# ConvFFN: tiles 2 to 20 of each half issued in a written-out order, with products summed in PSUM

## The chip, the cores and the metric

The kernel runs on one core of one Trainium2 chip. The metric is device time: microseconds from the first to the last instruction of one execution, as the median of several runs. A second number appears throughout, the span of one execution that the hardware profiler recorded.

## What is computed

The reference is a two-layer backbone over 1024 latent tokens of width 1024 and, in layer 0, 256 context tokens. Layer 0 mixes by Fourier transforms and a gated MLP, layer 1 by neighbourhood attention; both then run the same ConvFFN, which is where the change lies:

```python
def conv_ffn(h, w_up, conv_w, conv_b, w_down):
    L = h.shape[1]
    a = h @ w_up
    gate, val = a[..., :D_FF], a[..., D_FF:]
    gp = jnp.pad(gate, ((0, 0), (CONV_W // 2, CONV_W // 2), (0, 0)))
    g = gp[:, 0:L] * conv_w[0] + gp[:, 1:1 + L] * conv_w[1] + gp[:, 2:2 + L] * conv_w[2] + conv_b
    return (jax.nn.silu(g) * val) @ w_down
```

`D_FF` is 2816, the convolution is three wide, and layer 0 applies the ConvFFN to latent and context tokens, layer 1 to latent tokens alone. Everything is float32.

## The kernel before

**Precision.** Every float32 matrix is split into a high part (a copy rounded to the matmul's type, made on ScalarE, L447) and a low part (the difference, L448, on VectorE or, where the caller asks, on GpSimd). A product of two matrices is then three matmuls: high by high, high by low, low by high (`PASSES`).

**Halves and tiles.** The tokens of a layer are worked in two halves: in layer 0 two times 320 and two times 324 columns, in layer 1 two times 256 and two times 258. So there are four halves in the program, called the first to the fourth here. For each half the 22 tiles of 128 channels of `D_FF` follow each other (f = 0 to 21). The two-column-block product `h @ w_up` is done by a scheme with seven products P1 to P7 in place of eight. Each is 12 matmuls (four depths, three passes) with weight combinations called A00, A01, A11, S1 to S4 and operand combinations that were made before the half begins. After the products, their sums give four blocks: C0 = (c00, c01), the gate, and C1 = (c10, c11), the value.

**One tile.** `up` issues, for tile f: the seven products (L306), each into a PSUM bank of its own from a pool of eight named `pq`; a copy of P1 to SBUF on ScalarE (L323); seven additions on VectorE that take a product out of PSUM (L311); then `gate` (L315 on ScalarE, the outer taps of the convolution L317 and L319 on VectorE, silu L321 on ScalarE); the multiplication by the value (L361, VectorE); and the split of the result `act` (L447 and L448). Between the products stand four calls of `down` (L376), the second matrix multiplication for the pair of tiles before, with its accumulation into the residual stream (L382, VectorE). In a half of 256 columns a `down` is six matmuls 512 wide, in the others twelve.

**Weights.** The weights of tile f+1 are prepared while tile f runs. Two 512 KB loads (L236, queue of SyncE) bring A00 and A01 in one buffer, A10 and A11 in the other; these `wr` buffers are two in all, so that the loads for tile f+2 wait until all that is left in them of tile f+1 has been read. GpSimd forms the combinations in place: L241 (S1 = A10 + A11, needs both halves of the second load), L247 (S3 = A00 - A10), L248 (S2 = S1 - A00, overwrites A00) and L251 (S4 = A01 - S2). Each of the seven then gets its high part on ScalarE and its low part on VectorE, except A00, A01 and A11, whose low parts GpSimd makes too (`POOL`). Each weight has one slot in SBUF, which comes free when its product of tile f is done: A00 and S2 share the tile `wh` of one number, S1 and S4 that of another; A01, S3 and A11 are `wq`. `prep` does the same for the weights of `down` (`wd`).

**What sets the order.** The program is written in one order and put into another by a planner that simulates the engines and issues by priority. The sums, the gate and the split of `act` run at high priority. The planner's order is then fixed for each engine: each engine works through its own list, and waits where an operand is not there. During tiles 1 to 3 of a half further work lies between the products (`BESIDE`): in the first half of each layer the normalization of the second half's columns, one step being a VectorE instruction (L152), a ScalarE one (L153) and a store to DRAM (L176, `nd`) from one shared buffer; in layer 0's second half sums of squares.

## Time and profile before

| what | value |
|---|---|
| median of three runs | 2914.65 us (2911.54 to 2923.23) |
| the profiled execution's own time | 2920.99 us |
| its span | 2919.1 us |
| granted TensorE clock, mean | 0.974 |
| busy share: PE, PEld, DVE, ACT, POOL | 95%, 86%, 76%, 45%, 43% |
| gate (L315) of tile 2 in the four halves | 552.6, 1003.0, 2171.4, 2557.0 us |
| gate of tile 20 in the four halves | 911.3, 1363.4, 2479.2, 2877.7 us |

PE is TensorE's matmuls, PEld its weight loads, DVE VectorE, ACT ScalarE, POOL GpSimd, SP SyncE. Busy times of PE are modelled at their ends, so a PE that is always busy need not be at its peak. A row of the timeline gives start, duration, engine, line, output and inputs; a bracket gives the idle time before it and what ended it. A tile's period is the distance between two executions of L315, of which each tile has one: 88 in all.

### The profile page before, as it was taken

What the parts mean: (1) busy time and instruction counts of PE and PEld (TensorE: products, weight loads), DVE (VectorE), ACT (ScalarE), POOL (GpSimd) and SP (SyncE); (2) the same over time, 40 slices, a digit from 0 to 9 for tenths busy, and PEclk for the clock granted to TensorE, in tenths of its full rate; (3) what the DMA queues carried; (4) which work ended last, traced back from release to release, by engine and by line L of the source; (5) the groups of instructions that cost most, each with busy time, mean ns of one, the idle gap of its engine ahead of it and who ended that gap; (6) DMA issues with size and microseconds to landing.
All of it is one profiled execution on the core that took longest, in us unless ns stands there. A gap on an engine that the chain in (4) does not pass through costs nothing.

```text
span 2919.1 us, 47590 instructions
## 1 busy us (share of the span) xinstructions
...
## 2 busy tenths in 40 slices
...
GB/s 303 215 189 118 98 217 72 112 74 86 80 87 101 75 80 87 73 81 87 24 169 101 137 109 183 180 179 80 37 109 101 95 87 98 105 89 93 94 88 95
DMA packets 335886, 327.67 MB, mean 112 GB/s; under 512 B 16217, under 2 KB 264617, under 8 KB 335657
## 3 DMA queue, kind: packets, MB, share of 16 engines
...
## 4 chain that ended last, share of the span: by engine, by line
PE 61%; DVE 14%; DMA 7%; POOL 7%; issue 5%; ACT 5%; SPq 0%; POOLq 0%; DVEq 0%; ACTq 0%
PE pq L306 18%; PE pq L478 15%; PE pq L376 11%; PE ps L478 6%; DMA wr<-in_ffn_w_up_dram 4%; POOL ws L241 2%; DVE xl L382 2%; DVE wh L448 2%; PE pq L566 2%; POOL wh L448 2%; DVE hx L311 2%; PE ps L487 2%; ACT t L1227 1%; POOL wr L248 1%; DMA wd<-in_ada_w_dram 1%
## 5 line engine op out<-in xcount | busy, mean ns | idle before, releaser
L376 PE MATMUL pq<-act,wd 128*128 128x320 f32 (+3 forms) x3696 | 639.8, 322 | 59.3 <-DVE xl L382 24.5
L376 PEld LDWEIGHTS pq<-act,wd 128*128 128x128 f32 x3696 | 557.1, 193 | 92.0 <-DVE xl L382 28.7
L306 PE MATMUL pq<-hs,wh 128*128 128x320 f32 (+3 forms) x4128 | 607.5, 299 | 16.3 <-DVE xl L382 7.8
L306 PEld LDWEIGHTS pq<-hs,wh 128*128 128x128 f32 x4128 | 576.9, 191 | 26.4 <-DVE xl L382 11.2
L306 PE MATMUL pq<-hs,wq 128*128 128x320 f32 (+3 forms) x3144 | 469.8, 299 | 8.4 <-DVE wq L448 4.9
L478 PE MATMUL pq<-hs,wh 128*128 128x512 f32 (+3 forms) x2100 | 469.0, 358 | 3.6 <-DVE hs L724 1.9
L306 PEld LDWEIGHTS pq<-hs,wq 128*128 128x128 f32 x3144 | 442.5, 191 | 14.1 <-DVE wq L448 5.7
L478 PEld LDWEIGHTS pq<-hs,wh 128*128 128x128 f32 x2100 | 365.8, 193 | 78.0 <-issue 6.2
L241 POOL TENSOR_TENSOR ws<-wr 128x512 f32<-128x512 f32 x88 | 153.6, 1745 | 397.3 <-DMA wr<-in_ffn_w_up_dram 333.0
L447 ACT ACTIVATE wh<-wr 128x512 fp32r<-128x512 f32 (+1 forms) x223 | 161.8, 726 | 354.0 <-POOL wr L248 201.5
L382 DVE SCALAR_TENSOR_TENSOR xl<-pq,mod,xl 128x320 f32<-128x320 f32 (+5 forms) x616 | 304.1, 514 | 11.7 <-PE pq L376 11.6
L448 DVE TENSOR_TENSOR wh<-wr,wh 128x512 fp32r<-128x512 f32 (+1 forms) x147 | 166.9, 1135 | 184.8 <-ACT wh L447 184.5
L448 POOL TENSOR_TENSOR wq<-wr,wq 128x512 fp32r<-128x512 f32 x152 | 235.7, 1550 | 32.9 <-ACT wq L447 32.9
L478 PE MATMUL ps<-hs,wh 128*128 128x512 f32 x840 | 240.0, 405 | 3.6 <-ACT hs L721 1.8
L311 DVE TENSOR_TENSOR hx<-hx,pq 128x320 f32<-128x320 f32 (+3 forms) x440 | 196.1, 448 | 29.1 <-PE pq L306 21.6
L447 ACT ACTIVATE wq<-wr 128x512 fp32r<-128x512 f32 x262 | 160.0, 623 | 101.3 <-PE pq L306 73.2
L447 ACT ACTIVATE wh<-ws 128x512 fp32r<-128x512 f32 x172 | 107.5, 625 | 169.8 <-PE pq L306 115.4
L478 PEld LDWEIGHTS ps<-hs,wh 128*128 128x128 f32 x840 | 141.9, 191 | 41.6 <-issue 14.4
L251 POOL TENSOR_TENSOR ws<-wr 128x512 f32<-128x512 f32 x88 | 120.2, 1366 | 123.3 <-DVE wh L448 112.3
L999 POOL TENSOR_TENSOR hsp<-hsq,hsp 128x512 fp32r<-128x512 f32 (+1 forms) x40 | 47.1, 1185 | 265.5 <-ACT hsq L998 265.5
L1006 DVE RECIPROCAL hsq<-hsq 128x512 f32<-128x512 f32 (+1 forms) x40 | 121.1, 3030 | 52.9 <-ACT hsq L1005 52.1
L448 DVE TENSOR_TENSOR wd<-wrd,wd 128x512 fp32r<-128x512 f32 x176 | 155.5, 912 | 0.2 <-ACT wd L447 0.2
...
## 6 DMA issues: line engine op xcount, KB each, us to landing
wr<-in_ffn_w_up_dram SPq DMA_DIRECT2D x176, 512.0 KB, 4.4
...
adaw<-in_ada_w_dram SPq DMA_DIRECT2D x128, 256.0 KB, 3.6
...
```

The costliest lines, as they stand in the source:

```text
L241: op(raw["S1"], raw["A10"], raw["A11"], ALU.add)
L251: op(x, raw["A01"], raw["S2"], ALU.subtract)
L306: nc.tensor.matmul(o, w[wn][:, wp, k], self.part(s, bn, k, sp), start=(k == 0 and i == 0), stop=(k == 3 and i == 2))
L311: nc.vector.tensor_tensor(o, x, y, ALU.add)
L376: nc.tensor.matmul(pd, self.wds[j][i][:, wp, d % 4], self.acts[f][:, sp, lo:lo + m], start=(i == 0 and pi == 0), stop=(i == len(fs) - 1 an ...
L382: nc.vector.scalar_tensor_tensor(x, pd[:, a - lo:b - lo], net.mod[:, self.layer, st, 5, d:d + 1], x, ALU.mult, ALU.add)
L447: self.nc.scalar.activation(h, src, AF.Copy)
L448: return (e or self.nc.vector).tensor_tensor(l, src, f32(h), ALU.subtract)
L478: nc.tensor.matmul(o, w(wp, k), s(k, sp), start=(ki == 0 and pi == 0), stop=(ki == len(order) - 1 and pi == 2))
L487: nc.tensor.matmul(out, l[a], r[b], start=(first and i == 0), stop=(last and i == 2))
L566: nc.tensor.matmul(acc[32 * q:32 * q + 32, 0:256], self.sT[:, k, :], w[q // 2][:, 256 * (q % 2):256 * (q % 2) + 256], start=(k == 0), stop ...
L1006: nc.vector.reciprocal(r, r)
```

## The change

Tiles 2 to 20 of each half are taken out of the planner's hands for four engines (PE, DVE, ACT, POOL): inside the region each engine's list is the order in which the code issues, and that is read off a tuple of names, `STEADY` (or `STEADY2` for tile 2). The DMA queue of SyncE is not in the region. Inside it:

- P6 accumulates into P1's bank, P7 and (from tile 3) P4 go on in that bank, and P3 goes on in P5's. The running sums are copied out by ScalarE where they are wanted (`U`, `V`, `c10`), and three VectorE additions (`c00+`, `c11+`, `c01+`) are left of seven; tile 2 has four.
- The end of a tile (silu, multiplication, split of `act`) moves into the next tile, as do the last two accumulations of `down` (`X2`, `X3`): a name with a minus is work of the tile before.
- `D0` to `D3` are the matmuls of `down`, `X0` to `X3` their accumulations; `wA00` and so on are the steps of the weights. S1's parts are made before S2's, and the two loads stand behind S3's and A11's.
- A00's low part moves from GpSimd to VectorE.
- Tiles 0, 1 and 21 stay with the planner; the work beside tiles 2 and 3 is issued at its place between the products.

```diff
-    POOL = ("A00", "A01", "A11")
+    POOL = ("A01", "A11")
+    STEADY = ("P1", "silu-", "X2-", "X3-", "P2", "c00", "mul-", "wA00", "P6", "acth-", "c00+", "actl-", "wA01", "P5",
+              "U", "P7", "prep", "D0", "V", "wS1", "c11+", "P4", "wS2", "X0", "D1", "c10", "wS3", "wload0", "P3", "wA11",
+              "wload1", "X1", "D2", "c01+", "gate", "wS4", "taps", "D3", "ws")
+    STEADY2 = ("P1", "silu-", "P2", "c00", "mul-", "wA00", "P6", "acth-", "c00+", "actl-", "wA01", "P5",
+               "U", "P7", "prep", "V", "wS1", "c11+", "P4", "wS2", "c10+", "D0", "wS3", "wload0", "P3", "X0", "wA11",
+               "wload1", "D1", "c01+", "gate", "wS4", "X1", "D2", "taps", "D3", "ws")
...
+        def product(p, onto=None):
             wn, bn = self.PROD[p]
-            o = net.t(net.ps, [P, 512], "pq" if p in ("P2", "P5") else "pq")[:, :n]
+            o = net.t(net.ps, [P, 512], "pq")[:, :n] if onto is None else onto
             for k in range(4):
                 for i, (wp, sp) in enumerate(PASSES):
-                    nc.tensor.matmul(o, w[wn][:, wp, k], self.part(s, bn, k, sp), start=(k == 0 and i == 0),
-                                     stop=(k == 3 and i == 2))
+                    nc.tensor.matmul(o, w[wn][:, wp, k], self.part(s, bn, k, sp),
+                                     start=(onto is None and k == 0 and i == 0), stop=(k == 3 and i == 2),
+                                     skip_group_check=onto is not None)
...
+        if steady:
+            onto = dict(P6="P1", P7="P6", P3="P5")
+            if f > 2:
+                onto["P4"] = "P7"
+            ops = {"c00": lambda: copy(c00, x["P1"]), "c00+": lambda: add(c00, c00, x["P2"]),
+                   "U": lambda: copy(c01, x["P6"]), "V": lambda: copy(c10, x["P7"]),
+                   "c11+": lambda: add(c11, c10, x["P5"]), "c10": lambda: copy(c10, x["P4"]),
+                   "c10+": lambda: add(c10, c10, x["P4"]), "c01+": lambda: add(c01, c01, x["P3"]),
+                   "gate": gate, "taps": taps, "prep": prep}
+            i = 0
+            for tok in self.STEADY if f > 2 else self.STEADY2:
+                if tok in self.PROD:
+                    x[tok] = product(tok, x[onto[tok]] if tok in onto else None)
+                    if i in beside:
+                        beside[i]()
+                    i += 1
+                elif tok[0] == "D":
+                    adds["X" + tok[1]] = downs[int(tok[1])]()
+                elif tok[-1] == "-":
+                    if tok[:-1] in before:
+                        before[tok[:-1]]()
+                elif tok[0] == "X":
+                    adds.pop(tok)()
...
+            self.before = dict(after, **adds)
+            return
...
             for f in range(NF):
-                ups.append(self.up(s, f, hooks, [lambda d=d, j=f - 2: self.down(s, j, j % 2 * 4 + d) for d in range(4)]
+                if f == 2:
+                    region = self.net.tc.manual_schedule(engines={engines.PE, engines.DVE, engines.Activation, engines.Pool})
+                    region.__enter__()
+                if f == NF - 1:
+                    region.__exit__(None, None, None)
```

In the changed kernel the lines are: products L317, copies L326, additions L323, gate L329, taps L335 and L337, split of `act` L342 and L346, silu L347, multiplication L348, matmuls of `down` L437, accumulations L447, high and low parts of weights L523 and L524, GpSimd's sums L248, L254, L255 and L258.

**GpSimd, tile 14 of the fourth half.** Here stand the weights for the next tile; `ws` is S1 and then S4, `wr` the two raw buffers. Before:

```order
L241 TENSOR_TENSOR ws_27610<-wr_27556 128x512
L247 TENSOR_TENSOR wr_27556<-wr_27520,wr_27556 128x512
L448 TENSOR_TENSOR wh_20746<-wr_27520,wh_20746 128x512
L448 TENSOR_TENSOR wq_20648<-wr_27520,wq_20648 128x512
L248 TENSOR_TENSOR wr_27520<-ws_27610,wr_27520 128x512
L251 TENSOR_TENSOR ws_27610<-wr_27520 128x512
L448 TENSOR_TENSOR wq_20973<-wr_27556,wq_20973 128x512
```

After:

```order
L248 TENSOR_TENSOR ws_27275<-wr_27237 128x512
L254 TENSOR_TENSOR wr_27237<-wr_27221,wr_27237 128x512
L255 TENSOR_TENSOR wr_27221<-ws_27275,wr_27221 128x512
L524 TENSOR_TENSOR wq_20466<-wr_27221,wq_20466 128x512
L258 TENSOR_TENSOR ws_27275<-wr_27221 128x512
L524 TENSOR_TENSOR wq_20791<-wr_27237,wq_20791 128x512
```

Between the sum that gives S3 (L247, now L254) and the one that gives S2 (L248, now L255) stood two low parts, A00's (`wh`) and A01's (`wq`); now none stands there.

**VectorE, the end of tile 14 of the fourth half and the start of tile 15.** `hx` holds C0 and C1, `g` the gate, `xl` the residual stream. Before:

```order
L311 TENSOR_TENSOR hx_27616<-hx_27616,pq_27762 128x258
L448 TENSOR_TENSOR wh_20747<-ws_27610,wh_20747 128x512
L382 SCALAR_TENSOR_TENSOR xl_3274<-pq_27780,mod_127,xl_3274 128x256
L382 SCALAR_TENSOR_TENSOR xl_3274<-pq_27788,mod_127,xl_3274 128x258
L317 SCALAR_TENSOR_TENSOR g_27617<-hx_27616,cols_175_786,g_27617 128x515
L382 SCALAR_TENSOR_TENSOR xl_3409<-pq_27796,mod_127,xl_3409 128x256
L382 SCALAR_TENSOR_TENSOR xl_3409<-pq_27804,mod_127,xl_3409 128x258
L319 SCALAR_TENSOR_TENSOR g_27617<-hx_27616,cols_175_786,g_27617 128x515
L448 TENSOR_TENSOR wd_27866<-wrd_27668,wd_27866 128x512
L448 TENSOR_TENSOR wd_27869<-wrd_27668,wd_27869 128x512
L361 TENSOR_TENSOR g_27617<-g_27617,hx_27616 128x516
```

After:

```order
L323 TENSOR_TENSOR hx_27277<-hx_27277,pq_27334 128x258
L524 TENSOR_TENSOR wh_20565<-ws_27275,wh_20565 128x512
L335 SCALAR_TENSOR_TENSOR g_27278<-hx_27277,cols_175_786,g_27278 128x515
L337 SCALAR_TENSOR_TENSOR g_27278<-hx_27277,cols_175_786,g_27278 128x515
L447 SCALAR_TENSOR_TENSOR xl_3274<-pq_27440,mod_127,xl_3274 128x256
L447 SCALAR_TENSOR_TENSOR xl_3274<-pq_27447,mod_127,xl_3274 128x258
L447 SCALAR_TENSOR_TENSOR xl_3409<-pq_27460,mod_127,xl_3409 128x256
L447 SCALAR_TENSOR_TENSOR xl_3409<-pq_27467,mod_127,xl_3409 128x258
L348 TENSOR_TENSOR g_27278<-g_27278,hx_27277 128x516
L524 TENSOR_TENSOR wh_20564<-wr_27420,wh_20564 128x512
L323 TENSOR_TENSOR hx_27476<-hx_27476,pq_27496 128x258
L346 TENSOR_TENSOR act_27527<-g_27278,act_27527 128x516
```

The accumulations of the last two `down`s have moved behind both taps, the low parts of `wd` away from this place, and A00's low part (`wh_20564`) in behind the multiplication.

**ScalarE, the start of tile 15 of the fourth half, after the change.**

```order
L347 ACTIVATE g_27278<-g_27278 128x516
L326 ACTIVATE hx_27476<-pq_27478 128x258
L523 ACTIVATE wh_20564<-wr_27420 128x512
L342 ACTIVATE act_27527<-g_27278 128x516
L523 ACTIVATE wq_20466<-wr_27420 128x512
L326 ACTIVATE hx_27476<-pq_27478 128x258
```

The copy of P1 (first L326) stands behind silu of tile 14, and the copy of P1 + P6 (second L326) behind A00's high part, the high part of `act` and A01's high part. The matmuls of P6 write the bank that the first reads, those of P7 the bank that the second reads.

71 lines of the change are left out of this document (49 added, 22 removed).

## The prediction

> **What bounds the kernel now.** I first read the table of busy times by stretch. The stretches run from gate to gate: tile 2 of the first half, then tiles 4 to 19 of the first half and 3 to 19 of the others.
>
> ```profile
> core 0: us, PE busy (x) PEld busy (x) DVE busy (x) ACT busy (x) POOL busy (x), PEclk, DMA share, GB/s
> 552.60:579.50 26.90, 21.90 (x141) 20.85 (x140) 26.90 (x48) 12.44 (x24) 11.49 (x9) 0.98 0.36 104
> 599.80:911.30 311.50, 309.96 (x2109) 309.52 (x2108) 285.38 (x497) 128.18 (x208) 173.59 (x112) 1.00 0.27 82
> 1029.10:1363.40 334.30, 333.92 (x2237) 331.39 (x2237) 304.45 (x528) 137.99 (x223) 183.10 (x119) 1.00 0.27 81
> 2190.40:2479.20 288.80, 272.99 (x1848) 251.11 (x1847) 225.14 (x360) 123.94 (x221) 175.88 (x119) 0.98 0.32 94
> 2576.60:2877.70 301.10, 277.94 (x2233) 274.91 (x2232) 231.40 (x427) 125.84 (x223) 195.51 (x121) 0.98 0.30 90
> ```
>
> In layer 0 (second and third row) PE hardly has a gap: 309.96 of 311.50 us and 333.92 of 334.30. A tile takes 311.50 / 16 = 19.47 and 334.30 / 17 = 19.66 us there, and nothing that spares other engines can shorten it. In layer 1 a tile takes 288.80 / 17 = 16.99 and 301.10 / 17 = 17.71 us, and PE has gaps. Its floor there comes from stretches of the chain of waits in which PE alone runs, first the third half, then the fourth:
>
> ```profile
> 2303.33 2.79 PE pq L376 x12
> 2306.13 5.69 PE pq L306 x48
> ```
>
> ```profile
> 2752.82 5.79 PE pq L306 x48
> ```
>
> Third half: 84 x 5.69 / 48 + 24 x 2.79 / 12 = 9.96 + 5.58 = 15.54 us. Fourth: (84 + 48) x 5.79 / 48 = 15.92 us. The gap to the present periods, 1.45 and 1.79 us, times 17 tiles each, is 24.7 + 30.4 = 55 us: about all that the change can win in its long run of tiles.
>
> What holds layer 1 up is seen in the chain of waits of the fourth half, one lap of it:
>
> ```profile
> 2769.24 4.80 DMA wr<-in_ffn_w_up_dram
> ...
> 2774.17 3.44 POOL ws L241
> ...
> 2779.29 1.74 POOL wh L448
> 2781.03 0.06 POOL wq L448
> 2781.08 1.16 issue
> 2782.24 1.30 POOL wr L248
> ...
> 2787.30 4.94 DMA wr<-in_ffn_w_up_dram
> ```
>
> It is the weights' loop: load, GpSimd's sums, high part, low part, and the next load waits for the buffer. A lap is 2787.30 - 2769.24 = 18.06 us, the period of a tile. PE waits at its end for VectorE, which waits in its list for S2's high part.
>
> A second limit is less visible. GpSimd and VectorE shut each other out:
>
> ```profile
> 2765.63 1.27 POOL L251 TENSOR_TENSOR ws<-wr 128x512 f32<-128x512 f32 x1
> 2766.25 1.20 DVE L448 TENSOR_TENSOR wh<-wr,wh 128x512 fp32r<-128x512 f32 x1 [4.34 <-ACT wh L447]
> 2767.34 1.28 POOL L448 TENSOR_TENSOR wq<-wr,wq 128x512 fp32r<-128x512 f32 x1 [0.43 <-ACT wq L447]
> 2768.49 0.68 DVE L448 TENSOR_TENSOR wq<-wr,wq 128x512 fp32r<-128x512 f32 x1
> ```
>
> GpSimd's sum ends at 2766.90 and the low part that had begun at 2766.25 ends 0.55 us later; GpSimd's next ends at 2768.62, the other low part again 0.55 us later. So a low part needs 0.55 us with GpSimd kept out, and is held until GpSimd's running instruction (some 1.15 of its 1.28 us) is over. VectorE's additions out of PSUM show nothing of this (row of L311 below).
>
> The Trainium skill has the rule ("SBUF — State Buffer", Who interferes with whom): a VectorE instruction with two SBUF inputs contends with a GpSimd instruction that reads SBUF, by an exclusive lock. It speaks against this change, which takes off VectorE four additions that never collide and puts on one low part that does; the rows above agree, and what it would cost here is worked out, from rows, in the second and third rival.
>
> **The change, part by part.** TensorE's work is unchanged: as many matmuls, in fewer banks.
>
> *The loop.* Between S3's and S2's sums on GpSimd stood A00's and A01's low parts: 1.74 + 0.06 + 1.16 = 2.96 us of the lap. Both are gone from there, so the lap falls to 18.06 - 2.96 = 15.10 us, under the floor of 15.92. GpSimd's list loses 1.74 us of 195.51 / 17 = 11.5.
>
> *VectorE in layer 1.*
>
> ```profile
> L311 DVE TENSOR_TENSOR hx<-hx,pq 128x258 f32<-128x258 f32 x85 | 35.2, 414 | 1.2
> L448 DVE TENSOR_TENSOR wh<-ws,wh 128x512 fp32r<-128x512 f32 x35 | 30.7, 876 | 0.3 <-ACT wh L447 0.2
> L448 DVE TENSOR_TENSOR wh<-wr,wh 128x512 fp32r<-128x512 f32 x18 | 21.5, 1194 | 62.0 <-ACT wh L447 62.0
> L448 DVE TENSOR_TENSOR act<-g,act 128x516 fp32r<-128x516 f32 x17 | 16.8, 987 | 5.1 <-ACT act L447 5.1
> ```
>
> ```profile
> L315 ACT ACTIVATE g<-hx,cols,cols 128x516 f32<-128x516 f32 x17 | 13.9, 820 | 50.6 <-DVE hx L311 50.6
> L447 ACT ACTIVATE wh<-ws 128x512 fp32r<-128x512 f32 x35 | 21.9, 625 | 13.3 <-PE pq L306 6.5 <-POOL ws L241 6.2 <-POOL ws L251 0.6
> ```
>
> Busy now 231.40 / 17 = 13.61 us a tile in the fourth half. Four additions go (4 x 0.414 = 1.66), a low part comes (0.68): 12.63. New is a hole: between `c01+` and S4's low part nothing stands in VectorE's list, and it waits there for gate and S4's high part, 0.82 + 0.625 = 1.44 us: 14.07 with the collisions of today. Of those today's busy time holds about 2 x 0.20 + 0.51 + 0.31 = 1.2 us (the three means above less 0.68). Six GpSimd instructions remain; if none shut VectorE out it needs 12.9 us, if each did for its whole 1.15 us, 14.07 + 6.9 - 1.2 = 19.8. With half of that it needs 16.3, and in the third half (13.24 busy now) 16.0. Both lie just over PE's floor. I take the middle between floor and present period, 16.27 and 16.82 us, since two lists that are both nearly full also wait for each other: a gain of 0.72 and 0.89 us, times 17: **12.3 + 15.2 = 27.5 us**. The ends are 55 (floor) and nothing or a loss (rivals).
>
> ScalarE gets three copies more, 0.42 us each at most, on 125.84 / 17 = 7.4 us of a tile: covered in sum, but two of them are now waited for by PE. Before, a product went into a bank of its own; now P6 must wait until P1 is copied, P7 until P1 + P6 is.
>
> *Layer 0.* The price of that wait is a chain from the end of P3 to the start of P6 in the next tile: `c01+`, gate, S4's high and low part, four taps, silu, copy. Its rows, second half:
>
> ```profile
> L311 DVE TENSOR_TENSOR hx<-hx,pq 128x324 f32<-128x324 f32 x85 | 41.5, 488 | 10.1 <-PE pq L306 7.4
> L361 DVE TENSOR_TENSOR g<-g,hx 128x648 f32<-128x648 f32 x17 | 31.5, 1854 | 0.0
> L319 DVE SCALAR_TENSOR_TENSOR g<-hx,cols,g 128x131 f32<-128x131 f32 x17 | 15.5, 912 | 0.0
> L319 DVE SCALAR_TENSOR_TENSOR g<-hx,cols,g 128x515 f32<-128x515 f32 x17 | 14.8, 868 | 0.0
> L317 DVE SCALAR_TENSOR_TENSOR g<-hx,cols,g 128x515 f32<-128x515 f32 x17 | 12.7, 747 | 0.0
> L317 DVE SCALAR_TENSOR_TENSOR g<-hx,cols,g 128x131 f32<-128x131 f32 x17 | 6.0, 350 | 0.0
> ```
>
> ```profile
> 1003.05 0.93 ACT L315 ACTIVATE g<-hx,cols,cols 128x648 f32<-128x648 f32 x1 [0.71 <-DVE hx L311]
> 1009.92 0.75 ACT L321 ACTIVATE g<-g 128x648 f32<-128x648 f32 x1 [2.57 <-DVE g L319]
> 1013.69 0.42 ACT L323 ACTIVATE hx<-pq 128x324 f32<-128x324 f32 x1
> ```
>
> 0.49 + 0.93 + 0.63 + 0.68 + (0.75 + 0.87 + 0.35 + 0.91) + 0.75 + 0.42 = 6.78 us, and some 0.3 for seven handovers. What PE does meanwhile are D2, D3, P1 and P2, 48 x 333.92 / 2237 = 7.17 us. So the copy arrives as PE wants it, with nothing to spare. VectorE's sum there, 304.45 / 17 = 17.91 - 4 x 0.488 + 0.68 + 1.55 = 18.2 us, stays under 19.66; the slow row of L361 (1854 ns for 648 columns, where 512 of a low part take 680) shows that collisions of today, one of 1.0 us at least, are in it. I put 0.1 us a tile for chance meetings, 33 tiles: **+3 us**, from below zero by a few us (PE has no gap to give) up to the rival.
>
> *Tile 2 of the first and third half.* The normalization's steps stand fixed between the products and share one buffer, so each waits for the store of the one before:
>
> ```profile
> 555.17 0.72 ACT L153 ACTIVATE act<-act,mod 128x512 f32<-128x512 f32 x1 [1.08 <-DVE act L152]
> DMA to landing us min/median/max: 1.5/2.1/3.8
> ```
>
> After a step VectorE may do the next only 0.72 + 0.3 (issue) + 2.1 = 3.1 us later. Written between them are 1.2 us (`c00+`, `act`'s low part), 2.5 (two of `wd`, S1, `c11+`) and 1.9 (S2, `c10+`, S3): (3.1 - 1.2) + (3.1 - 2.5) + (3.1 - 1.9) = 3.7 us of waiting. VectorE is busy throughout that tile now (26.90 of 26.90), so it comes in full. Twice, and rounded up: **+8 us**; ends: nothing, if the planner's own order lost as much, and 5 x 3.1 in each, 31.
>
> **Sum.** -27.5 + 3 + 8 = -16.5 us. The profiled execution took 2920.99 us, 6.3 over the median of the runs; less 16.5 it would be 2904.5, and on the median's scale 2914.65 - 16.5 = **2898 us**.
>
> **Rivals.** *The tiles reach PE's floor*: GpSimd's instructions fall into VectorE's holes (the hole after `c01+` is one that fits), and nothing waits. For it: the lap of 15.1 is under the floor. Against it: VectorE's 14 to 16 us of 15.9. Time: 2914.65 - 55 + 8 = 2868.
>
> *A new wait of the same length*: in layer 1 VectorE, shut out, is late with `c01+`, silu comes late, PE stands before P6, P7 or D3 (whose bank waits for `c01+`) as long as it stood before `down`. For it: S1's and S2's low parts follow GpSimd's sums closely, as the row of 1194 ns shows for today. Time: 2914.65 + 8 + 3 = 2926, within 0.5% of before. Whether it or the forecast comes true hangs on the phases of the two lists, which no row shows.
>
> *Slower: layer 0's chain runs over.* The chain to P6 has nothing to spare, and `c01+` stands in the list behind S3's low part and `X1`. If GpSimd meets one more instruction of the chain than today's rows hold, by half its length, 0.58 us, every one of 33 tiles loses that: 19 us, with nothing won in layer 1 and 8 us in the tiles 2: 2914.65 + 27 = 2942. It decides once the chain takes longer than 7.2 us. For it: L361's 1854 ns, which shows GpSimd there; against it: GpSimd has one instruction less, and the multiplication is no part of this chain.
>
> **How the numbers follow.** Forecast (half of layer 1's gap) 0.33, floor reached 0.19, new wait of the same length 0.22, layer 0 longer 0.26. About 0.5% of this kernel, 15 us, is what a measurement tells from no change. Faster by more: the floor and most of the forecast (0.28), 0.47. Within: the rest of the forecast and the same-length wait, 0.05 + 0.20 = 0.25. Slower: 0.28. The forecast's own range is 2880 to 2915; with floor and longer chain it is 2852 to 2943.
>
> **What would show it.** Right: periods of L329 of 16.0 to 16.6 us in the third half and 16.4 to 17.2 in the fourth; GpSimd's wait for the load before the first sum still there, the wait of ScalarE for S2's sum gone; gaps of PE before L317 ended by the copies L326. Layer 0's tiles at 19.4 to 19.8. L159 waiting for stores `nd` in tile 2 of the first and third half. Wrong: layer 0 at 20 us or more (the chain), or layer 1 at 17 or more (the same wait under another name), or a period at 15.6 and 15.9 (floor).

## The result: 72 us slower, and the profile after

The changed kernel takes 2987.42 us (median of 4 runs, 2981.65 to 2989.14) against 2914.9 us before (4 runs beside it, 2911.54 to 2923.23): a ratio of 1.0241, with a 95% interval of 1.0215 to 1.0267. The forecast was 2898, its widest range 2852 to 2943. The profiled execution took 2989.14 us, span 2987.2 us, 68.1 more than before.

Where they came from is read from the gates of the profiled executions, four entries (gate of tile 0 to gate of tile 4) and four steady runs of 16 tiles (gate of tile 4 to gate of tile 20):

| stretch | before | after | difference |
|---|---|---|---|
| entries of the four halves, us | 80.6, 73.2, 65.1, 61.7 | 87.2, 86.2, 75.2, 66.6 | +34.6 |
| steady tile, layer 0, first and second half, us | 19.47, 19.73 | 20.66, 20.80 | +36.2 |
| steady tile, layer 1, third and fourth half, us | 17.13, 17.74 | 17.22, 17.36 | -4.6 |
| all else | | | +1.9 |

So three things want explaining: layer 0 lost a microsecond a tile, layer 1 won nothing, and each entry lost 5 to 13 us. First the busy times by stretch (columns as in the prediction), gate to gate in the long runs of the four halves, of the changed kernel:

```profile
611.10:941.70 330.60, 314.21 (x2114) 309.95 (x2113) 293.30 (x448) 137.66 (x256) 139.77 (x96) 1.00 0.26 77
1066.70:1423.10 356.40, 338.65 (x2246) 333.99 (x2245) 313.30 (x476) 148.24 (x274) 148.50 (x102) 1.00 0.25 76
2253.70:2546.70 293.00, 268.79 (x1837) 246.76 (x1836) 268.52 (x308) 137.37 (x273) 145.07 (x102) 1.00 0.31 92
2651.80:2946.50 294.70, 277.12 (x2252) 271.82 (x2251) 269.68 (x375) 137.56 (x273) 150.73 (x102) 1.00 0.30 90
```

In layer 0 PE, which had no gap, now has 16.4 and 17.8 us of them. In layer 1 VectorE has fewer instructions than before (308 against 360, 375 against 427) and is busy for longer: 268.52 us against 225.14, 269.68 against 231.40. Work was taken off it and its time went up.

The groups of the page name PE's releaser:

```profile
L317 PE MATMUL pq<-hs,wh 128*128 128x320 f32 (+3 forms) x4128 | 621.2, 304 | 129.0 <-ACT hx L326 123.5
L347 ACT ACTIVATE g<-g 128x640 f32<-128x640 f32 (+3 forms) x88 | 60.3, 685 | 282.3 <-DVE g L337 282.3
```

123.5 us of idle time before the products end with one of ScalarE's copies (L326), the wait for P1 to be copied before P6 may go on in its bank; and ScalarE stands for the last tap (L337) before silu (L347), which precedes that copy in its list. The chain of waits shows one lap of it, a steady tile of the second half:

```profile
1275.92 1.06 PE pq L317 x7
...
1277.00 0.50 DVE hx L323
...
1278.36 0.62 ACT wh L523
...
1279.01 0.69 DVE wh L524
1279.70 0.68 DVE g L335
...
1280.40 0.76 DVE g L337
1281.16 1.31 DVE g L335
...
1282.50 1.35 DVE g L337
...
1283.93 0.74 ACT g L347
1284.67 0.34 ACT hx L326
...
1285.05 2.05 PE pq L317 x12
```

From P3's end (1276.98) to P6 (1285.05) it is 8.07 us. PE has 7.1 us of work meanwhile and stands 0.97 us. The two taps of 131 columns take 1.31 and 1.35 us in this chain; in the profile before they took 0.35 and 0.91. The timeline of the same lap shows what holds them:

```profile
1280.50 1.81 POOL L248 TENSOR_TENSOR ws<-wr 128x512 f32<-128x512 f32 x1 [4.10 <-DVE g L335]
1281.08 1.39 DVE L335 SCALAR_TENSOR_TENSOR g<-hx,cols,g 128x131 f32<-128x131 f32 x1
1282.39 1.29 POOL L254 TENSOR_TENSOR wr<-wr,wr 128x512 f32<-128x512 f32 x1
1282.50 1.34 DVE L337 SCALAR_TENSOR_TENSOR g<-hx,cols,g 128x131 f32<-128x131 f32 x1
```

GpSimd's L248 ends at 1282.31 and the tap that began at 1281.08 ends 0.16 us later; L254 ends at 1283.68 and the next tap again 0.16 us later. GpSimd's instructions pass between the taps, and each makes a short tap last as long as itself.

In 33 of the 34 tiles between gate 3 and gate 20 of layer 0's two halves two of the four taps are held so. In 16 they are the two short ones, as in the lap shown; in 17, 11 of them in the second half, GpSimd starts one tap earlier and holds the second wide tap and the first short one. The means of the second half mix both kinds:

```profile
L335 DVE SCALAR_TENSOR_TENSOR g<-hx,cols,g 128x515 f32<-128x515 f32 x17 | 12.7, 749 | 0.0
L337 DVE SCALAR_TENSOR_TENSOR g<-hx,cols,g 128x515 f32<-128x515 f32 x17 | 23.8, 1402 | 0.6
L335 DVE SCALAR_TENSOR_TENSOR g<-hx,cols,g 128x131 f32<-128x131 f32 x17 | 23.5, 1382 | 0.0
L337 DVE SCALAR_TENSOR_TENSOR g<-hx,cols,g 128x131 f32<-128x131 f32 x17 | 11.9, 700 | 0.6
```

In layer 1 the groups of the third half (gate 3 to gate 20), first of the changed kernel:

```profile
L524 DVE TENSOR_TENSOR wh<-wr,wh 128x512 fp32r<-128x512 f32 x34 | 59.7, 1756 | 0.0
L524 DVE TENSOR_TENSOR wd<-wrd,wd 128x512 fp32r<-128x512 f32 x34 | 41.6, 1264 | 0.0
L346 DVE TENSOR_TENSOR act<-g,act 128x512 fp32r<-128x512 f32 x17 | 29.2, 1716 | 0.0
L524 DVE TENSOR_TENSOR wh<-ws,wh 128x512 fp32r<-128x512 f32 x34 | 23.3, 686 | 23.9 <-ACT wh L523 23.9
```

The four groups are the same operation with the same width. Undisturbed it takes 0.69 us (fourth row); `wd`'s low parts take 1.26, `act`'s 1.72, A00's and S2's 1.76. VectorE is busy 268.52 / 17 = 15.80 us of a tile and waits 23.9 / 17 = 1.41 us for S4's high part: 17.21, the period of 17.23. Its list has no other room, so it sets the tile.

At an entry, the stretch from gate 1 to gate 2 takes 24.5, 23.6, 23.9 and 21.2 us, where it took 14.6, 12.6, 13.2 and 12.1. Timelines of PE and ScalarE in the fourth half, and then busy times in pieces from the same place:

```profile
2619.18 5.53 PE L317 MATMUL pq<-hs,wh 128*128 128x258 f32 x24 [6.75 <-ACT hx L326]
```

```profile
2618.22 0.63 ACT L347 ACTIVATE g<-g 128x516 f32<-128x516 f32 x1 [1.91 <-DVE g L337]
2618.76 0.37 ACT L326 ACTIVATE hx<-pq 128x258 f32<-128x258 f32 x1
```

```profile
2619.20:2622.00 2.80, 2.80 (x13) 2.80 (x14) 1.68 (x4) 1.67 (x3) 0.00 (x0) 0.50 0.68 196
2622.00:2625.00 3.00, 3.00 (x16) 3.00 (x16) 2.24 (x3) 1.42 (x3) 2.51 (x2) 0.50 0.03 5
2625.00:2628.00 3.00, 3.00 (x26) 3.00 (x26) 1.53 (x2) 1.54 (x4) 2.92 (x3) 0.97 0.18 49
```

It is the same wait, here 6.75 us long: P1's copy of tile 2 stands behind the silu of tile 1, which waits for all of tile 1's sums, gate and taps. The same wait stands in the other three entries, with 9.03, 8.10 and 12.32 us (first to third half); the longest gap of PE at the four entries before was 2.48, 2.20, 4.23 and 1.28 us. In all, PE's idle time in the entries rises from 26.7 to 54.2 us. And a gap costs more than its length: for the next 5.8 us the granted clock is 0.50, some 27 matmuls run in them (the rows count those at a bound twice), which would take some 3.2 us at the pace of the 3 us after, so by this estimate some 2.6 us are lost on top.

### The profile page after: what moved, and what is told of

The parts are those of the page before. It is cut to its first block, busy times and chain, and to the rows that moved or that the text cites. A ratio compares the mean times of both kernels' runs of the same rounds, so it can differ in the third digit from the quotient of the medians.

```text
span 2987.2 us, 46943 instructions
## 1 busy us (share of the span) xinstructions
PE 2777.9 (93%) x17978; PEld 2523.0 (84%) x17978; DVE 2306.2 (77%) x3524; ACT 1354.4 (45%) x2672; POOL 1107.9 (37%) x968
## 4 chain that ended last, share of the span: by engine, by line
PE 52%; DVE 29%; ACT 8%; issue 6%; DMA 4%; POOL 1%; SPq 0%; ACTq 0%; DVEq 0%; POOLq 0%
PE pq L317 15%; PE pq L554 15%; PE pq L437 7%; PE ps L554 6%; DVE wh L524 6%; DVE g L337 4%; DVE g L335 3%; DVE xl L447 3%; DVE wd L524 2%; DVE hx L323 2%; DVE wq L524 2%; ACT wh L523 2%; PE pq L642 2%; PE ps L563 2%; ACT t L1303 1%
## 5 line engine op out<-in xcount | busy, mean ns | idle before, releaser
L317 PE MATMUL pq<-hs,wh 128*128 128x320 f32 (+3 forms) x4128 | 621.2, 304 | 129.0 <-ACT hx L326 123.5
L317 PEld LDWEIGHTS pq<-hs,wh 128*128 128x128 f32 x4128 | 584.1, 194 | 152.5 <-ACT hx L326 141.4
L437 PE MATMUL pq<-act,wd 128*128 128x320 f32 (+3 forms) x3696 | 611.3, 317 | 9.9 <-DVE xc L447 3.6
L437 PEld LDWEIGHTS pq<-act,wd 128*128 128x128 f32 x3696 | 548.1, 190 | 31.8 <-ACT act L342 4.2
L317 PE MATMUL pq<-hs,wq 128*128 128x320 f32 (+3 forms) x3144 | 468.7, 297 | 8.0 <-DVE wq L524 2.7
L317 PEld LDWEIGHTS pq<-hs,wq 128*128 128x128 f32 x3144 | 437.9, 190 | 13.2 <-ACT hx L326 3.6
L524 DVE TENSOR_TENSOR wh<-wr,wh 128x512 fp32r<-128x512 f32 (+1 forms) x223 | 299.3, 1342 | 73.3 <-ACT wh L523 73.0
L447 DVE SCALAR_TENSOR_TENSOR xl<-pq,mod,xl 128x320 f32<-128x320 f32 (+5 forms) x616 | 292.5, 511 | 12.5 <-PE pq L437 12.5
L248 POOL TENSOR_TENSOR ws<-wr 128x512 f32<-128x512 f32 x88 | 124.6, 1416 | 426.1 <-DMA wr<-in_ffn_w_up_dram 314.0
L524 POOL TENSOR_TENSOR wq<-wr,wq 128x512 fp32r<-128x512 f32 x152 | 236.5, 1556 | 106.4 <-ACT wq L523 106.4
L326 ACT ACTIVATE hx<-pq 128x320 f32<-128x320 f32 (+3 forms) x312 | 125.8, 403 | 240.6 <-PE pq L317 164.7
L523 ACT ACTIVATE wh<-wr 128x512 fp32r<-128x512 f32 (+1 forms) x223 | 161.3, 723 | 141.2 <-PE pq L554 73.9
L524 DVE TENSOR_TENSOR wd<-wrd,wd 128x512 fp32r<-128x512 f32 x176 | 206.9, 1212 | 12.8 <-ACT wd L523 12.8
L524 DVE TENSOR_TENSOR wh<-ws,wh 128x512 fp32r<-128x512 f32 x172 | 124.1, 721 | 114.3 <-ACT wh L523 114.3
L347 ACT ACTIVATE g<-g 128x640 f32<-128x640 f32 (+3 forms) x88 | 60.3, 685 | 282.3 <-DVE g L337 282.3
L255 POOL TENSOR_TENSOR wr<-ws,wr 128x512 f32<-128x512 f32 x88 | 122.4, 1390 | 163.3 <-DVE wh L524 154.7
L258 POOL TENSOR_TENSOR ws<-wr 128x512 f32<-128x512 f32 x88 | 116.5, 1323 | 165.5 <-DVE wh L524 150.2
L329 ACT ACTIVATE g<-hx,cols,cols 128x640 f32<-128x640 f32 (+3 forms) x88 | 76.7, 871 | 218.5 <-DVE hx L323 216.1
```

The lines of the kernel that those rows point to most:

```text
L248: op(raw["S1"], raw["A10"], raw["A11"], ALU.add)
L255: op(x, raw["S1"], x, ALU.subtract)
L258: op(x, raw["A01"], raw["S2"], ALU.subtract)
L317: nc.tensor.matmul(o, w[wn][:, wp, k], self.part(s, bn, k, sp), start=(onto is None and k == 0 and i == 0), stop=(k == 3 and i == 2), skip ...
L326: nc.scalar.activation(o, x, AF.Copy)
L437: nc.tensor.matmul(pd, self.wds[j][i][:, wp, d % 4], self.acts[f][:, sp, lo:lo + m], start=(i == 0 and pi == 0), stop=(i == len(fs) - 1 an ...
```

## The experiments

Three questions: is the wait for the copies the cause in layer 0 and at the entries; what fills VectorE in layer 1; and which of the change's parts does good or harm. Where each kernel stands (ratios to the kernel before, run on the same chip; entries and tiles are from one profiled execution of each; entries are the sum over four halves; for comparison, they are 280.6, 19.47, 19.73, 17.13, 17.74 before and 315.2, 20.66, 20.80, 17.22, 17.36 after):

| kernel | us | ratio, 95% interval | entries | steady tile in the four halves |
|---|---|---|---|---|
| copy_first | 2968.8 | 1.0175 (1.0158 to 1.0192) | 308.0 | 20.33, 20.41, 17.15, 17.54 |
| taps_first | 2930.9 | 1.0045 (1.0028 to 1.0061) | 307.2 | 19.38, 19.56, 17.16, 17.25 |
| short_sums | 2893.1 | 0.9924 (0.9909 to 0.9938) | 299.2 | 19.38, 19.55, 15.54, 16.62 |
| lowpart_alone | 2886.1 | 0.9899 (0.9884 to 0.9914) | 279.9 | 19.34, 19.57, 16.09, 17.08 |
| fixed_order | 2917.8 | 1.0000 (0.9983 to 1.0017) | 300.9 | 19.32, 19.55, 17.15, 17.36 |
| fixed_less_gpsimd | 2906.2 | 0.9964 (0.9951 to 0.9978) | 297.5 | 19.34, 19.56, 16.59, 16.72 |
| planner_no_lowparts | 2892.6 | 0.9923 (0.9895 to 0.9952) | 280.5 | 19.46, 19.57, 16.81, 17.35 |
| own_banks | 2982.2 | 1.0244 (1.0207 to 1.0281) | 313.1 | 20.57, 20.78, 17.60, 17.50 |
| beside_early | 2927.5 | 1.0027 (1.0015 to 1.0038) | 300.2 | 19.33, 19.56, 17.17, 17.27 |
| a00_back | 2965.3 | 1.0164 (1.0136 to 1.0192) | 312.3 | 20.14, 20.39, 16.68, 17.68 |
| planner_a11_only | 2883.1 | 0.9873 (0.9856 to 0.9889) | 279.6 | 19.32, 19.57, 16.26, 16.78 |
| interleaved | 2883.8 | 0.9894 (0.9876 to 0.9911) | 292.7 | 19.38, 19.56, 16.01, 16.28 |
| interleaved_beside | 2876.2 | 0.9867 (0.9850 to 0.9883) | 286.4 | 19.38, 19.55, 16.04, 16.28 |
| interleaved_own_banks | 2897.1 | 0.9944 (0.9925 to 0.9962) | 299.6 | 19.37, 19.54, 16.60, 16.63 |

### Layer 0: the chain to P6

**copy_first.**

```diff
-    STEADY = ("P1", "silu-", "X2-", "X3-", "P2", "c00", "mul-", ...
+    STEADY = ("P1", "c00", "silu-", "X2-", "X3-", "P2", "mul-", ...
-    STEADY2 = ("P1", "silu-", "P2", "c00", "mul-", ...
+    STEADY2 = ("P1", "c00", "silu-", "P2", "mul-", ...
```

> The changed kernel, with ScalarE's copy of P1 (L326) taken out from behind the silu of the tile before: it now stands ahead of it in ScalarE's list, in tile 2 too. Nothing is left out. Theory A (the loss is PE's wait before P6 for that copy, which hangs on the end of the tile before): in the profile of the change PE stood 123.5 us before L317 with ScalarE's L326 as the releaser, and nothing but its place in the list keeps the copy. Layer 0's tiles fall from 20.7 to 20.8 us to 19.5 to 19.8 (33 tiles, about -35 us), the gaps of 7 to 14 us at the entry of the four regions shrink (about -20 us), and the time is 2905 to 2935. Theory B (VectorE's list is the bound, the copy only shows it): the wait moves on to P7, which needs the second copy U behind silu and the high part of act, or to D0, and a tile of layer 0 stays at 20.4 or more; the time is 2965 to 2990.

2968.8 us: theory B's range. The wait before P6 is gone from the steady tiles, and another stands before P7. PE and ScalarE in a tile of the second half, two timelines:

```profile
1204.82 2.05 PE L317 MATMUL pq<-hs,wq 128*128 128x324 f32 x12 [0.69 <-ACT hx L326]
```

```profile
1203.18 0.75 ACT L342 ACTIVATE act<-g 128x648 fp32r<-128x648 f32 x1 [1.51 <-DVE g L348]
1203.83 0.61 ACT L523 ACTIVATE wq<-wr 128x512 fp32r<-128x512 f32 x1
1204.35 0.42 ACT L326 ACTIVATE hx<-pq 128x324 f32<-128x324 f32 x1
```

The second copy (`U`, 1204.35) stands behind `act`'s high part, which waits for the multiplication, which waits for silu: the late chain of the tile before reaches PE by the next copy. Taking away one wait on a chain that is late only moves it, and 0.33 and 0.39 us are won of the 1.19 and 1.07 that a tile had lost.

**taps_first.**

```diff
-              "wload1", "X1", "D2", "c01+", "gate", "wS4", "taps", "D3", "ws")
+              "wload1", "X1", "D2", "c01+", "gate", "taps", "wS4", "D3", "ws")
```

(and in `STEADY2` likewise).

> The changed kernel, with the taps (L335, L337) ahead of S4's parts instead of behind them, on VectorE and ScalarE; the copy of P1 stays behind silu. Nothing is left out. Theory A (the chain from P3's end to P6 is too long by about 1 us in layer 0): S4's high and low part, 0.62 + 0.69 us, leave the chain, it falls from 8.07 to about 6.8 us against 7.17 us of cover, and layer 0's tiles go to 19.6 to 19.9 (about -33 us); the entry of the regions does not change (the copy still stands behind silu): 2945 to 2960. Theory B (GpSimd's two sums shut VectorE out wherever the taps stand; they start when the loads have landed): the earlier taps are free of them and S4's low part is hit in their place, the same time for the tile as in A, but P3 of the next tile or the list behind it comes late, and the tile stays over 20.3: 2970 to 2990.

2930.9 us, 57 less than the changed kernel, and layer 0 at 19.38 and 19.56, better than theory A said. Groups of the second half (gate 3 to gate 19), then a row of the table of waits there (us in total, times, longest):

```profile
L337 DVE SCALAR_TENSOR_TENSOR g<-hx,cols,g 128x131 f32<-128x131 f32 x16 | 5.7, 355 | 0.6
L335 DVE SCALAR_TENSOR_TENSOR g<-hx,cols,g 128x131 f32<-128x131 f32 x16 | 5.6, 350 | 0.0
```

```profile
POOL ws L248 <- DVE wh L524: 85.1, 17, 5.0
```

Both short taps take 0.35 us. They are free because L248 writes the buffer that S4's low part reads (`ws`, one buffer): with S4's low part behind the taps, GpSimd cannot begin its next sums before them, and waits 5.0 us instead. So the chain lost 0.62 + 0.69 us of S4 and, against the lap shown above, (1.31 - 0.35) + (1.35 - 0.355) = 1.96 us of collisions. The stretch from gate 1 to gate 2 stays in three halves, as expected (24.6, 23.5 and 23.8 us), and falls to 19.3 in the fourth. The entries as a whole got 8.0 us shorter, 5.3 of them in the second half, which was not expected; no run here shows why.

**short_sums.** This kernel leaves out most of S1 and S3 in tiles 2 to 20 (8 of 128 columns of each block are summed; the rest of S1 is filled with zeros).

```diff
-            op(raw["S1"], raw["A10"], raw["A11"], ALU.add)
+            c = 8 if self.busy else P
+            if self.busy:
+                nc.gpsimd.memset(raw["S1"], 0.0)
+            op(raw["S1"][:, :, :c], raw["A10"][:, :, :c], raw["A11"][:, :, :c], ALU.add)
...
-                op(raw["A10"], x, raw["A10"], ALU.subtract)
+                c = 8 if self.busy else P
+                op(raw["A10"][:, :, :c], x[:, :, :c], raw["A10"][:, :, :c], ALU.subtract)
```

> The changed kernel, with two of GpSimd's sums cut short in tiles 2 to 20: L248 (S1 = A10 + A11, after a fill with zeros that reads nothing) and L254 (S3) are made for 8 of 128 columns of each block only, so most of S1 and S3 is wrong; waits and order are those of the change. If GpSimd's running sums are what holds VectorE at the last two taps, the 131-wide L335 and L337 fall from 1.31 to 1.39 and 1.34 to 1.76 us to 0.35 to 0.4, the chain from P3 to P6 from 8.07 to about 6.1 us, PE's wait before P6 in layer 0 goes and its tiles take 19.5 to 19.8 (about -35 us); layer 1 gains too, 0.3 to 0.8 us a tile. Time 2925 to 2950. If the taps are long for another reason, they stay over 1 us and the time stays at 2975 to 2990.

2893.1 us, below the range, since layer 1 gained more than expected (1.68 and 0.74 us a tile) and the entries got 16 us shorter, which was not expected at all. Layer 0, in the unchanged order, is at 19.38 and 19.55. The short taps (here L339 and L341) in the groups of the second half:

```profile
L341 DVE SCALAR_TENSOR_TENSOR g<-hx,cols,g 128x131 f32<-128x131 f32 x17 | 6.0, 355 | 0.6
L339 DVE SCALAR_TENSOR_TENSOR g<-hx,cols,g 128x131 f32<-128x131 f32 x17 | 5.9, 345 | 0.0
```

That is the cause in layer 0 by itself: without GpSimd's two long sums, and with S4 still in the chain, the taps are short (the second wide one too, 0.78 us for 1.40) and PE waits 0.3 us for the copies where it waited 17.8. In layer 1's third half the tile falls to 15.54 us, PE's floor as the prediction worked it out.

### Which part does what

**lowpart_alone.**

```diff
-    POOL = ("A00", "A01", "A11")
+    POOL = ("A01", "A11")
```

in the kernel before.

> The kernel before, with A00's low part moved from GpSimd to VectorE and nothing else: the planner orders everything. Nothing is left out. Theory A (in layer 1 the weights' loop sets the tile, a lap of 18.06 us in the fourth half with 2.96 us of low parts between two sums): about 1.3 us of the lap go, layer 1's tiles gain 0.3 to 1 us each (34 tiles: -10 to -34 us), layer 0 stays since PE has no gap there: 2880 to 2905. Theory B (VectorE's list, 13.6 us busy, is as full with its collisions): the low part put on it meets GpSimd, and the gain is eaten: 2910 to 2930.

2886.1 us, theory A: one name moved makes the kernel before 1.0% faster. Layer 1's tiles are 1.04 and 0.66 us shorter, 16 x (1.04 + 0.66) = 27 us, as much as the forecast gave the whole change there; layer 0 and the entries stay. So the rest of the change, order and sums in PSUM together, costs 2987 - 2886 = 101 us.

**a00_back**, the other way round: the changed kernel with `POOL = ("A00", "A01", "A11")`.

> The changed kernel with A00's low part back on GpSimd, in the written order; nothing else. Nothing is left out. Theory A (turns: a low part costs the pair of engines 1.3 us on GpSimd and 0.68 on VectorE): layer 1's tiles rise from 17.2 and 17.4 to 17.6 to 18.3 us (34 tiles: +10 to +30 us), layer 0's stay at 20.5 to 21.2 (the chain): 2995 to 3020. Theory B (VectorE's own list sets the tile): VectorE has 0.7 to 1.3 us less, layer 1's tiles fall to 16.2 to 16.8: 2950 to 2975.

2965.3 us: theory B's range, but neither theory's pattern. The third half is faster (16.68 for 17.22), the fourth slower (17.68 for 17.36), layer 0 faster by 0.4 to 0.5. "A low part costs less on VectorE" is no rule of its own: in the planner's order its move to VectorE gains in both halves of layer 1, in the written one it loses 0.54 us a tile in the third half and gains 0.32 in the fourth. What counts is where the two engines' instructions meet.

**own_banks.** Seven banks, seven additions, in the written order:

```diff
-            onto = dict(P6="P1", P7="P6", P3="P5")
-            if f > 2:
-                onto["P4"] = "P7"
+            onto = {}
-                   "U": lambda: copy(c01, x["P6"]), "V": lambda: copy(c10, x["P7"]),
+                   "U": lambda: add(c10, x["P6"], c00), "V": lambda: add(c10, c10, x["P7"]),
+                   "c01": lambda: add(c01, x["P5"], c10),
```

(`c01` is issued after P5, `U` now ahead of `c00+`, and `c10+` in the place of `c10`.)

> The changed kernel without sums in PSUM: each product has a bank of its own again, and VectorE makes the seven additions of before, at the places of the copies U, V and c10. All else is the written order of the change. Nothing is left out. Theory A (the order, with VectorE's low parts close behind GpSimd's instructions, and not the sums in PSUM, costs the time in layer 1 and in layer 0's steady tiles): PE's waits for copies go, at the entry too (-6 us in each half), but VectorE gets 4 x 0.49 us in layer 0 and 4 x 0.41 us in layer 1 on a list that is 92% busy: layer 0's tiles at 20.6 to 21.2, layer 1's at 18.2 to 18.8: 3000 to 3025. Theory B (the sums in PSUM, which tie P6 and P7 to copies, are the damage): with banks of their own the products run ahead, layer 0's tiles at 19.6, layer 1's at 16.5 to 17.2: 2900 to 2940.

2982.2 us, in neither range, and not to be told from the changed kernel (2981.0 to 2993.7 against 2981.7 to 2989.1). Theory B falls: with the sums in PSUM and their waits for copies gone, the written order is as slow. In layer 0 another limit of the same length stands in the chain's place, VectorE's own list. Busy times of the second half (gate 3 to gate 20):

```profile
1059.80:1413.00 353.20, 341.81 (x2255) 338.53 (x2254) 324.42 (x544) 129.61 (x222) 152.59 (x102) 0.99 0.25 77
```

VectorE is busy for 324.42 of 353.20 us, where it was for 313.30 of 356.40; 26.8 us more are its wait for S4's high part, so its list has hardly any room left. The short taps are held here as well (1.39 and 1.27 us). In layer 1 theory A over-priced the four additions: a tile is 0.38 and 0.14 us longer, not 1 to 1.4.

**planner_no_lowparts** (`POOL = ()` in the kernel before) and **planner_a11_only** (`POOL = ("A11",)`).

> The kernel before with all three low parts moved from GpSimd to VectorE, everything in the planner's order. Nothing is left out. Theory A (turns, as in fixed_less_gpsimd): beyond the gain of lowpart_alone (30 us) another 10 to 20 us in layer 1, layer 0 at PE's floor as before: 2865 to 2880. Theory B (lowpart_alone gained by the shorter lap of the weights' loop alone, and the four additions more that VectorE has here leave no room): VectorE at 17.9 + 3 x 0.68 = 19.9 us in layer 0's tiles, over 19.5; layer 0 slower by 0.3 to 0.5 us a tile, layer 1 no better than lowpart_alone: 2890 to 2915.

> The kernel before with A00's and A01's low parts moved to VectorE and A11's left on GpSimd, in the planner's order: between lowpart_alone (2886 us, layer 1's tiles 16.1 and 17.1) and planner_no_lowparts (2893 us, 16.8 and 17.4). Nothing is left out. Theory A (the shorter lap and the turns both matter, and VectorE's list becomes the limit only with the third): 2878 to 2888. Theory B (VectorE's list is the limit from the second on): 2886 to 2898.

2892.6 and 2883.1 us. With the second low part moved, layer 1's tile gains 0.30 us in the fourth half and loses 0.17 in the third; with the third moved too it loses in both. So theory A of the latter holds in its range, and of the former it falls (2892.6 us lies in B's); but layer 0 stays at PE's floor in all three (19.3 to 19.6), so B's reason is half wrong too. The gain is in the first.

### The entries

**fixed_order.** Copies and taps moved together:

```diff
-    STEADY = ("P1", "silu-", "X2-", "X3-", "P2", "c00", "mul-", "wA00", "P6", "acth-", "c00+", "actl-", "wA01", "P5",
-              "U", "P7", ...
+    STEADY = ("P1", "c00", "silu-", "X2-", "X3-", "P2", "mul-", "wA00", "P6", "U", "acth-", "c00+", "actl-", "wA01", "P5",
+              "P7", ...
-              ... "c01+", "gate", "wS4", "taps", "D3", "ws")
+              ... "c01+", "gate", "taps", "wS4", "D3", "ws")
```

(and `STEADY2` likewise).

> The changed kernel with three moves in its two tuples: the copy of P1 ahead of silu, the copy U right behind P6 (ahead of the high part of act), the taps ahead of S4's parts. Nothing is left out. Theory A (the entry of a region is dear because PE, after P1 and P2 of tile 2, stands before P6 for the copy behind tile 1's silu, and with the copy alone moved stands before P7 for U): both copies now hang on P1 and P6 only; the stretch from gate 1 to gate 2 falls from 21 to 24 us by 4 to 8 us in each half, layer 0's tiles stay at the 19.4 to 19.6 of taps_first, layer 1's at 17.2 (VectorE's list sets them): 2895 to 2915. Theory B (the entry is dear because tile 1's gate comes late, and tile 2's VectorE work behind it): the gap only moves to D0 or P4, and the time is 2920 to 2935.

2917.8 us, as long as the kernel before and between the two theories' ranges. Gate 1 to gate 2 takes 24.1, 23.2, 23.2 and 17.8 us: only the fourth half, the one that has no work beside its tiles, comes near theory A, with 3.4 us less than in the changed kernel.

**beside_early.** All work beside the tiles goes to tile 1, two steps at each product:

```diff
-    BESIDE = {1: (1, 3, 6), 2: (1, 2, 4, 5, 6), 3: (1, 2, 4, 5, 6)}
+    BESIDE = {1: range(7)}
-                                   {i: lambda: next(norm, None) for i in self.BESIDE.get(f, ())}))
+                                   {i: lambda: (next(norm, None), next(norm, None)) for i in self.BESIDE.get(f, ())}))
```

> The order of fixed_order, with the work that lay beside tiles 1 to 3 of a half (normalization steps, sums of squares) put wholly beside tile 1, which the planner orders: two steps at each of its seven products, none inside the written region. Nothing is left out. Theory A (in the written lists each such step has VectorE, ScalarE and a store or a GpSimd addition wait for each other, and the copies P6 and P7 hang on queue behind it on ScalarE): the stretch from gate 1 to gate 2, 24.1, 23.2 and 23.2 us in the first three halves of fixed_order, falls to 15 to 19 us, near the 17.8 of the fourth half, which has no such work; tile 1 gets 2 to 5 us longer; time 2895 to 2908. Theory B (the entry is dear because the written lists begin only when all of tile 1's list is through): these stretches stay at 21 or more, time 2912 to 2930.

The stretches fall to 21.2, 17.8, 17.9 (and 17.7): theory A's mechanism in the second and third half, most of the way. The entries' sum stays all the same (300.2 for 300.9): what the first and third half win (5.4 and 5.7 us) the second loses, since the sums of squares, all in tile 1, make that tile 32.7 us long instead of 14.0. The time, 2927.5, lies in theory B's range. That it is 10 us over fixed_order is not the steps' doing as far as the profiled executions show: there the entries and the steady tiles are the same within 0.1 us a tile, and 9.7 us lie between the second half's tile 20 and the third half's tile 0 (776.4 for 766.7 us), a stretch that the edit does not touch and that takes 765 to 777 us over the kernels here.

### Layer 1: where VectorE's instructions meet GpSimd's

**fixed_less_gpsimd.** `POOL = ()` in fixed_order.

> The order of fixed_order, and A01's and A11's low parts on VectorE as well: GpSimd keeps its four sums only. Nothing is left out. Theory A (in layer 1 VectorE and GpSimd take turns, and the sum of both sets the tile: a low part costs 1.3 us of it on GpSimd and 0.68 on VectorE): layer 1's tiles fall from 17.2 to 16.0 to 16.6 us (34 tiles: -20 to -40 us), layer 0 stays at 19.4 to 19.6: 2870 to 2890. Theory B (VectorE's own work sets the tile, its list gets 1.36 us longer): layer 1's tiles rise to 17.8 to 18.5, layer 0's to 19.8 to 20.4: 2940 to 2970.

2906.2 us, layer 1 at 16.59 and 16.72. VectorE got two low parts more, and its tile became shorter by 0.56 and 0.64 us: so it is not the number of VectorE's instructions that sets the tile. The edit also shortens GpSimd's list by two instructions; that the turns and not this list decide is shown only by interleaved below, which leaves GpSimd's instructions as they are. Theory A by its sign; its size was at the edge (16.0 to 16.6), the time outside the range. Theory B falls.

What the turns look like in fixed_order, in the timeline of a tile of the third half:

```profile
2265.99 1.29 POOL L248 TENSOR_TENSOR ws<-wr 128x512 f32<-128x512 f32 x1 [5.60 <-DMA wr<-in_ffn_w_up_dram]
2266.19 1.64 DVE L348 TENSOR_TENSOR g<-g,hx 128x512 f32<-128x512 f32 x1
2267.35 1.62 POOL L254 TENSOR_TENSOR wr<-wr,wr 128x512 f32<-128x512 f32 x1
2267.75 1.78 DVE L524 TENSOR_TENSOR wh<-wr,wh 128x512 fp32r<-128x512 f32 x1
2269.67 1.27 POOL L255 TENSOR_TENSOR wr<-ws,wr 128x512 f32<-128x512 f32 x1 [0.69 <-DVE wh L524]
2269.78 1.71 DVE L346 TENSOR_TENSOR act<-g,act 128x512 fp32r<-128x512 f32 x1
```

When the load lands, GpSimd starts a string of four instructions, and VectorE's list has its operations with two SBUF inputs there, back to back. Each waits a whole GpSimd instruction (L248 ends at 2267.28, the multiplication at 2267.83, 0.55 us later). VectorE's accumulations of `down`, which take an input out of PSUM, had run just before, while GpSimd stood idle for 5.60 us. The next kernel moves them.

**interleaved.** Same instructions, other places for X2, X3, `c00+` and X0:

```diff
-    STEADY = ("P1", "c00", "silu-", "X2-", "X3-", "P2", "mul-", "wA00", "P6", "U", "acth-", "c00+", "actl-", "wA01", "P5",
-              "P7", "prep", "D0", "V", "wS1", "c11+", "P4", "wS2", "X0", "D1", ...
+    STEADY = ("P1", "c00", "silu-", "P2", "mul-", "X2-", "wA00", "P6", "U", "acth-", "X3-", "actl-", "c00+", "wA01", "P5",
+              "P7", "prep", "D0", "V", "wS1", "c11+", "X0", "P4", "wS2", "D1", ...
```

> The order of fixed_order with four of VectorE's names moved in the steady tuple: X2 and X3 (accumulations out of PSUM), which ran before the multiplication, now stand between the multiplication, A00's low part and act's low part, c00+ behind act's low part, and X0 ahead of S2's low part, where GpSimd's sums run. Same instructions, nothing left out. Theory A (layer 1's tile is set by VectorE's operations with two SBUF inputs, which stand back to back where GpSimd's four instructions run, while its additions out of PSUM run where GpSimd is idle): the additions run during GpSimd's instructions and VectorE loses less of each; layer 1's tiles fall from 17.15 and 17.36 us to 15.6 to 16.6 and 15.9 to 16.8 (-20 to -50 us), layer 0 stays at 19.3 to 19.6: 2865 to 2900. Theory B (GpSimd's instructions follow VectorE's wherever these stand, since they wait for them): the collisions stay as many, tiles of layer 1 stay at 17.0 to 17.5: 2905 to 2925.

2883.8 us, theory A: layer 1's tiles at 16.01 and 16.28, 34 us less than fixed_order in all. Busy times of third and fourth half (gate 3 to gate 20), and groups of the third (gate 4 to gate 20):

```profile
2193.30:2465.10 271.80, 266.42 (x1825) 242.41 (x1825) 242.26 (x307) 139.06 (x272) 162.60 (x103) 1.00 0.33 99
2566.50:2838.60 272.10, 269.53 (x2210) 266.30 (x2209) 246.45 (x371) 136.64 (x268) 160.78 (x102) 1.00 0.32 96
```

```profile
L524 DVE TENSOR_TENSOR wh<-wr,wh 128x512 fp32r<-128x512 f32 x32 | 30.2, 943 | 0.0
L524 DVE TENSOR_TENSOR wd<-wrd,wd 128x512 fp32r<-128x512 f32 x32 | 50.5, 1616 | 0.0
L524 DVE TENSOR_TENSOR wh<-ws,wh 128x512 fp32r<-128x512 f32 x32 | 37.2, 1163 | 0.0
L346 DVE TENSOR_TENSOR act<-g,act 128x512 fp32r<-128x512 f32 x16 | 13.6, 851 | 3.3 <-ACT act L342 3.3
```

The same number of instructions as in the changed kernel takes VectorE 242.26 us instead of 268.52, and 246.45 instead of 269.68. `act`'s low part fell from 1.72 to 0.85 us, A00's and S2's from 1.76 to 0.94. Not all collisions are gone: `wd`'s low parts rose from 1.26 to 1.62 us, S1's and S4's from 0.69 to 1.16. The balance is 1.55 us a tile less of VectorE's time in the third half.

**interleaved_own_banks**: the edit of own_banks on top of it.

> interleaved without sums in PSUM: seven products in seven banks and seven additions on VectorE, as before, in the same written order. Nothing is left out. It measures what the sums in PSUM are worth once the order is not at fault. Theory A (VectorE sets the tile of layer 1, and an addition out of PSUM costs its length): layer 1's tiles longer by up to 4 x 0.41 us than in interleaved, by 0.8 to 1.6 us, layer 0 within 0.3 us of PE's floor of 19.4: 25 to 55 us slower than interleaved. Theory B (the additions hide in the time in which GpSimd shuts VectorE's other operations out, or PE sets the tile): within 10 us of interleaved.

2897.1 us, 13 more than interleaved, between the theories: 0.59 and 0.35 us a tile in layer 1, none in layer 0. That is what the sums in PSUM are worth where the order lets them.

**interleaved_beside**: interleaved, with the normalization steps of the first and third half beside tile 1.

```diff
-                                   {i: lambda: next(norm, None) for i in self.BESIDE.get(f, ())}))
+                                   {i: lambda: [next(norm, None) for _ in range(1 + (s == 0))]
+                                    for i in (self.BESIDE.get(f, ()) if s else range(7) if f == 1 else ())}))
```

> interleaved, with the normalization steps of the first and third half put wholly beside tile 1, two at each product (the sums of squares of the second half stay where they are, since moving them cost tile 1 18.7 us in beside_early). Nothing is left out. Theory A (the steps, on queues written out, hold the copies back in tile 2): the stretch from gate 1 to gate 4 of the first and third half falls by 5 us each against interleaved: 8 to 12 us faster than it. Theory B (the steps cost the same wherever they stand): within 4 us of interleaved.

2876.2 us (2874.53 to 2878.14; interleaved 2879.9 to 2891.3), 7.6 us less: just short of theory A's range, above B's. The entries of the first and third half are 3.5 and 3.0 us shorter; the stretch from gate 1 to gate 4, of which theory A spoke, falls by 4.1 and 1.5 us where it had said 5 each. It is the fastest kernel of this study, 1.3% under the kernel before; planner_a11_only, at 0.9873, can't be told from it by the ratios.

## Why the prediction was wrong, point by point

**Layer 0 (forecast +3, measured +36 in the steady tiles).** The place, the mechanism and the point from which it decides were those of the last rival: the chain from P3 to P6 has 7.17 us of cover, and decides past 7.2. The failed step is the term "four taps": 0.75 + 0.87 + 0.35 + 0.91 = 2.88 us, taken from the rows of before. In these GpSimd meets chiefly the last tap (0.91 us where an unhindered one takes 0.35); the sum takes them as they are and puts 0.1 us for anything more. After the change they take 0.749 + 1.382 + 1.402 + 0.700 = 4.23 us in the second half (means of the groups), 4.10 in the lap shown, and the chain is 8.07 us for a forecast of 7.1. "Against it: GpSimd has one instruction less" was the wrong question; when GpSimd starts decides, and that is set by S4's low part (it frees `ws`) and the load. The rival's price was half a GpSimd instruction, 0.58 us a tile. The taps went up by 4.23 - 2.88 = 1.35 us, and 1.19 and 1.07 us of a tile were lost. taps_first and short_sums show it from two sides.

**Layer 1 (forecast -27.5, measured -4.6 in the 16 steady tiles).** The forecast gain was there to be had: lowpart_alone, which takes A00's low part alone out of the loop, gets 27 us, with tiles of 16.09 and 17.08 us where 16.27 and 16.82 had been forecast. That two halves miss in opposite directions makes the fit of their sum in part luck, and that the lap falls to 15.10 us is shown by no run: in the fourth half of lowpart_alone A01's low part (1.74 us) still stands between the two sums. The failed step is VectorE's collisions. "With half of that it needs 16.3, and in the third half 16.0": it needs 17.2 in the third half, 15.80 busy and 1.41 waiting. Beside the 13.7 us that the same working gives with the collisions of today (13.24 - 4 x 0.41 + 0.68 + 1.44), that is 3.5 us for 2.3. It is no chance meeting that averages to a half: the load starts GpSimd's string at the same point of each tile, and the written order has VectorE's operations with two SBUF inputs at that point. interleaved shows it, with the same instructions in 16.01 us. It was the second rival for layer 1 ("a new wait of the same length"), and the phases that "no row shows" were indeed what decided.

The rule of the Trainium skill that the prediction weighed ("SBUF — State Buffer", Who interferes with whom) was the right one to fear, and the trace agrees with it: every long row above is a VectorE operation with two SBUF inputs beside a GpSimd instruction that reads SBUF, and no addition out of PSUM is longer than before (0.41 us in layer 1 and 0.48 to 0.49 in layer 0, in both kernels).

**Entries (forecast +8, measured +34.6).** The failed step is the term "3.7 us of waiting" for the stores of the normalization steps, in tile 2 of two halves, as the only cost of an entry. That wait did not come: in the changed kernel VectorE waits once for a store at each of the two entries, 0.5 and 1.0 us. The main term was left out: the first P6 of the region waits for a copy that stands behind the end of tile 1, 6.75 us in the fourth half, which has no such steps at all, and 8.1 to 12.3 us in the others, and PE's clock is halved for 5.8 us behind the gap in the fourth half. The prediction looked at this wait only in the steady tile.

The experiments say how far this goes. Moving copies and taps together gives 14.3 of the 34.6 us back (fixed_order), interleaved another 8.2, and taking the normalization steps out of the region 6.3 (interleaved_beside): the size of the forecast term, by another wait than it named. The 5.8 us that are left in interleaved_beside are mostly the second half's, 4.6 us above the kernel before. Its sums of squares still lie in tiles 2 and 3, and they hold a copy back: in fixed_order ScalarE's L718 there waits 3.10 us for GpSimd's addition of squares (L720), the copy `U` stands behind it, and PE waits 3.36 us for that. beside_early, without them in the region, has 56.6 us from gate 1 to gate 4 of that half, for 65.4 in fixed_order and 57.3 before. How the rest divides is open.

**The signs that were named.** The periods of 17 us or more in layer 1 and 20 or more in layer 0 stood in the list of what would show the forecast wrong; both came. Right were that PE's gaps end with L326, that the wait for the load before GpSimd's first sum stays (89.0 us in the third half), and that ScalarE's wait for S2's sum goes (67.5 us in the third half before, none after). Of the signs for a right forecast the periods did not come, nor, but for the two short ones above, the waits for stores in tile 2.
